# Small float32 products of three mixers, written so that neighbours stand in different column groups of the PE array

## The chip, the cores and the metric

The kernel runs on one NeuronCore of a Trainium2 chip. The metric is the device time of one execution in microseconds, the median over runs.

The engines that matter: TensorE (PE) multiplies, with its weight loads recorded apart (PEld); VectorE (DVE) and ScalarE (ACT) work on rows of 128 partitions; GpSimd (POOL) does little here; SyncE (SP) issues the DMAs. Each engine works through its own queue in order.

## The reference

Two layers; each has a half-step SwiGLU block, a mixer of three branches, a cross-attention and another half-step SwiGLU block. The sequence is 256 tokens of width 1024, all in float32. Of the mixer:

```
gla: a = where(lower, (q*eg) @ (k/eg).T, (q/eg) @ (k*eg).T)     4 heads of 32, chunks of 64 tokens
     o = a @ v + (q*eg) @ S_prev ;  S = decay * S + k.T @ v
s5:  x_t = Abar x_{t-1} + Bbar u_t ;  y_t = Re(C x_t) + D u_t    16 groups of 16 channels, 64 states
fox: p = softmax(q k.T / 8 + F_t - F_s, causal) ; o = p @ v      8 heads of 64, query blocks of 128
```

## The kernel before

Every large product is done in float32r by a high and a low part in three passes (`mm3`, L255). A weight block of 128x1024 (`wf`) is fetched by SP, split by ACT into the high part (`wh`, L237) and by DVE into the low part (`wl`, L241); seven split blocks form a ring, and `ahead` keeps it filled up to six or seven blocks ahead of PE.

The mixers and the set-up of S5 are generators, *tasks*, that are moved one step on at `tick`, `rest` or `run_tasks`, between the projections that PE works on. A `yield` ends a step. No scheduler moves instructions: their order on each engine is that in which the Python code writes them.

The small products that the change touches are plain float32 matmuls. A matmul writes to the PSUM partitions that its output tile names; partitions 0 to 31, 32 to 63, 64 to 95 and 96 to 127 belong to four column groups of the array. One such matmul stands in the program as one instruction, and in the trace as two records on PE and two on PEld.

- **S5 set-up** (`s5_setup`, during the first SwiGLU block): for each of eight pairs of groups, `cz.T @ wa` (L744), 32x128, the real and the imaginary part accumulated. All outputs stand at partitions 0 to 31, four pairs to a PSUM bank (`mm`). DVE transposes each bank in blocks of 32 into `hk` (L746), adds the D term (`dd`, L626), and four ACT copies (L753) spread `hk` over the four partition blocks of `m1`, which the mixer reads.
- **GLA** (`gla`): for each pair of chunks `pr`, the logits of a chunk (L858, two products of 64x256: `kie` with `qb[0]`, `keg` with `qb[1]`), the even chunk at partitions 0 to 63 and the odd at 64 to 127 of one bank. Then the output `po` (L884 from the state, 64x256, not for chunk 0; L887 four heads, 64x64 with 64 rows of the array), again by chunks.
- **FoX** (`fox`): seven steps for four heads. Step s does the values of head s-3 (L1071, L1072: keys 0 to 127 for all 256 queries, keys 128 to 255 for the last 128), the transposes of the softmax of head s-2 (L1059) and the logits of head s (L1040, L1041). Even heads write to partitions 0 to 63, odd ones to 64 to 127 of one bank, which is split after the odd head. A layer runs `fox` twice.

Of the kernel before, what the change touches and what calls it, by code (L numbers as in the profile page):

```python
# [8 lines left out]
F32 = mybir.dt.float32  # L9
# [24 lines left out]
WARM = 6  # L34
TAIL = 5

C_ID, C_FM, C_P2, C_HM, C_END = 0, 128, 512, 520, 524


PASSES = ((0, 0), (0, 1), (1, 0))  # L40
# [14 lines left out]
class Trunk:  # L55
# [554 lines left out]
    def s5_setup(self, l, pool):  # L610
# [8 lines left out]
        n = [0]  # L619
# [5 lines left out]
        def tt(o, x, y, op, eng=V):  # L625
            eng.tensor_tensor(o, x, y, op=op)  # L626
            return o
# [108 lines left out]
            tt(m3[:, i], (w1, w2)[i], (w2, w1)[i], (ALU.add, ALU.subtract)[i])  # L736
            yield

        hk = pool.tile([128, 8, 4, 32], F32, tag="hk", name="hk")[0:32]
        for q in range(2):  # L740
            ps = self.bank()
            for j in range(4):
                for i in range(2):
                    T.matmul(ps[0:32, j * 128:(j + 1) * 128], lhsT=cz[:, i, 4 * q + j],  # L744
                             rhs=wa[:, i, 4 * q + j].rearrange("p k h -> p (k h)"), start=i == 0, stop=i == 1)
            V.transpose(hk[:, 4 * q:4 * q + 4].rearrange("p a k h -> p (a k h)"), ps[0:32])  # L746
            yield
        dd = pool.tile([128, 8, 32], F32, tag="dd", name="dd")[0:32]
        tt(dd, self.ident[0:32, 0:32].unsqueeze(1).to_broadcast([32, 8, 32]),
           col[0:32, 32:40].unsqueeze(2).to_broadcast([32, 8, 32]), ALU.mult)  # L750
        tt(hk[:, :, 3], hk[:, :, 3], dd, ALU.add)
        for s in range(4):
            S.copy(m1[32 * s:32 * s + 32, :, 0:4 - s], hk[:, :, s:4])  # L753
        yield

        er, ei = self.er, self.ei
        V.memset(er[:, :, 0:1], 1.0)
# [60 lines left out]
    def gla(self, l, psm, vg, sgg, com, pool):  # L818
        yield from self.gla_gates(l, psm, com, pool)
        yield  # L820
        qs, ks = self.qk
        nc, ident = self.nc, self.ident
        V, S, G, T = nc.vector, nc.scalar, nc.gpsimd, nc.tensor
        eg, ieg, kd = self.ge

        def tl(shape, name):
            return pool.tile(shape, F32, tag=name, name=name)


        hm = self.cst[:, C_HM:C_HM + 4]  # L830
        kie, keg, ae = tl([128, 256], "g"), self.zeu[0][:, 0:256], tl([128, 3], "ae")
        V.tensor_tensor(kd, ks, kd, op=ALU.mult)
        V.tensor_tensor(kie, ks, ieg, op=ALU.mult)
        V.tensor_tensor(keg, ks, eg, op=ALU.mult)
        S.copy(ae, eg[:, 63:255:64])
        yield 2
        pkt = self.pbank(1)
        for t in range(2):
            T.transpose(pkt[:, t * 128:(t + 1) * 128], kd[:, t * 128:(t + 1) * 128], ident)
        kdt = tl([128, 512], "zl")[:, 0:256].rearrange("p (a b) -> p a b", a=2)  # L840
        S.copy(kdt, two(pkt[:, 0:256]))
        yield
        qb = []
        for e in (eg, ieg):
            V.tensor_tensor(e, qs, e, op=ALU.mult)
            qb.append(self.per.tile([128, 4, 256], F32, tag="nw", name="qb", bufs=2))
            V.tensor_tensor(qb[-1], e[:].unsqueeze(1).to_broadcast([128, 4, 256]),
                            hm.unsqueeze(2).to_broadcast([128, 4, 256]), op=ALU.mult)
            yield
        qf = eg  # L850
        asel = two(self.zeu[1])
        for pr in range(2):
            at = self.pbank(pr)
            for c in (2 * pr, 2 * pr + 1):
                o = slice(64 * (c % 2), 64 * (c % 2) + 64)
                cc = slice(c * 64, c * 64 + 64)
                for i, k in ((0, kie), (1, keg)):
                    T.matmul(at[o, i * 256:(i + 1) * 256], lhsT=k[:, cc], rhs=qb[i][:, :, cc], start=True, stop=True)  # L858
            S.copy(asel[:, pr], at[:, 256:512])
            V.copy_predicated(asel[:, pr], self.gmask, at[:, 0:256])  # L860
            yield

        st = [self.zeu[0][:, 0:256], self.zeu[0][:, 256:512], tl([128, 256], "g")]
        pds = self.pbank(0), self.pbank(1)
        for c in range(3):
            r = slice(64 * (c % 2), 64 * (c % 2) + 64)
            T.matmul(pds[c % 2][:, (c // 2) * 256:(c // 2) * 256 + 256], lhsT=kdt[r, c // 2], rhs=vg[r, c // 2],
                     start=True, stop=True)
        hm = hm.unsqueeze(2).to_broadcast([128, 4, 64])
        for c in range(3):  # L870
            s4 = st[c].rearrange("p (h e) -> p h e", h=4)
            V.tensor_tensor(s4, pds[c % 2][:, (c // 2) * 256:(c // 2) * 256 + 256].rearrange("p (h e) -> p h e", h=4), hm,
                            op=ALU.mult)
            if c:
                V.scalar_tensor_tensor(st[c], st[c - 1], ae[:, c:c + 1], st[c], op0=ALU.mult, op1=ALU.add)
        po = self.pbank(3)
        ggain = tl([128, 256], "scan0")
        nc.sync.dma_start(ggain, self.a["gla_norm_g"][l].partition_broadcast(128))
        yield
        for c in range(4):  # L880
            r = slice(64 * (c % 2), 64 * (c % 2) + 64)
            o = po[r, (c // 2) * 256:(c // 2) * 256 + 256]
            if c:
                T.matmul(o, lhsT=qf[:, c * 64:c * 64 + 64], rhs=st[c - 1], start=True, stop=False)  # L884
            for h in range(4):
                e = slice(h * 64, h * 64 + 64)
                T.matmul(o[:, e], lhsT=asel[r, c // 2, e], rhs=vg[r, c // 2, e], start=c == 0,  # L887
                         stop=c == 0 or h == 3)
            if c == 1:
                yield  # L890
        osq, on = tl([128, 512], "zl"), self.zeu[0]
        o8 = osq[:].rearrange("p (a b) -> p a b", a=8)
        S.activation(osq, po, AF.Square)
        ov, orr = tl([128, 8], "ov"), tl([128, 8], "orr")
        V.tensor_tensor(sgg, sgg, ggain[:].unsqueeze(1).to_broadcast([128, 2, 256]), op=ALU.mult)
        V.tensor_reduce(ov, o8, axis=AX.X, op=ALU.add)
        V.tensor_scalar(ov, ov, 1.0 / 64.0, EPS, op0=ALU.mult, op1=ALU.add)
        G.tensor_tensor(orr, ov, self.mhalf, op=ALU.pow)
        yield
        V.tensor_tensor(o8, po[:].rearrange("p (a b) -> p a b", a=8), orr[:].unsqueeze(2).to_broadcast([128, 8, 64]),  # L900
                        op=ALU.mult)
        V.scalar_tensor_tensor(on, osq, 0.5, sgg[:].rearrange("p a b -> p (a b)"), op0=ALU.mult, op1=ALU.mult)
        yield 2
        pot = self.pbank(3)
        for t in range(2):
            for k in range(2):
                T.transpose(pot[:, k * 256 + t * 128:k * 256 + t * 128 + 128],
                            on[:, t * 256 + k * 128:t * 256 + k * 128 + 128], ident)
        goh = com.tile([128, 2, 256], F32R, tag="goh", name="goh")
        gol = com.tile([128, 2, 256], F32R, tag="gol", name="gol")  # L910
        self.split_ps(goh, gol, pot)
        self.gla_out = (goh, gol, 2)
# [115 lines left out]
    def fox(self, q, fqk, fv, out, pool):  # L1028
# [31 lines left out]
            pts[i] = tl([128, 512], "ptn")[:, 0:384]  # L1060
            S.copy(pts[i], pt[:, 0:384])

        pf = [None]

        def value(i):
            if i % 2 == 0:
                pf[0] = self.bank()
            o = pf[0][64 * (i % 2):64 * (i % 2) + 64]
            c = slice((4 * q + i) * 64, (4 * q + i) * 64 + 64)
            p = pts.pop(i)  # L1070
            T.matmul(o[:, 0:256], lhsT=fv[:, 0, c], rhs=p[:, 0:256], start=True, stop=False)  # L1071
            T.matmul(o[:, 128:256], lhsT=fv[:, 1, c], rhs=p[:, 256:384], start=False, stop=True)  # L1072
            if i % 2:
                hp = (4 * q + i) // 2
                self.split_ps(out[0][:, hp], out[1][:, hp], pf[0][:, 0:256])

        for s in range(7):
            if s >= 3:
                value(s - 3)
            if 2 <= s < 6:  # L1080
                turn(s - 2)
            if s < 4:
                logits(s)
                self.n_logits = s + 1
            yield
            if s < 4:
                scale(s)
# [339 lines left out]
def _layout(inp):  # L1427
# [56 lines left out]

    pair = [4 * (j % 2) + j // 2 for j in range(8)]
    col = np.zeros((L, 128, 40), np.float32)
    col[:, 0:32, 32:40] = f["s5_d"].reshape(L, 8, 32)[:, pair].transpose(0, 2, 1)
    col[:, :, 2:4] = f["s5_glu_b"].reshape(L, 2, 128).transpose(0, 2, 1)
    col[:, :, 4] = f["gla_gate_b"]
    col[:, 32:40, 5] = f["fox_f_b"]  # L1490
# [19 lines left out]
        cst[:, C_FM + c:C_FM + c + 128] = np.where(r[:, None] >= r[None, :], 0.0, -NEG)  # L1510
    o["scan0"] = (np.arange(256) % 64 != 0).astype(np.float32)
    cst[:, C_P2:C_P2 + 8] = (2.0 ** np.arange(8))[None, :]
    cst[:, C_HM:C_HM + 4] = r[:, None] // 32 == np.arange(4)[None, :]
    o["cst"] = cst
    o["gmask"] = np.ascontiguousarray(
# [26 lines left out]
```

## Time and profile before

| | us |
|---|---|
| median of 3 runs | 1439.51 |
| lowest and highest run | 1436.96, 1439.73 |
| profiled execution, its own time | 1437.95 |
| span of its trace | 1436.1 |
| PE busy | 1419.9 (99%) |
| DVE busy | 927.3 (65%) |
| ACT busy | 712.9 (50%) |

The span runs from the first to the last instruction in the trace; the profiled execution's own time is 1.85 us longer. Busy time of PE is the union of its records, whose ends are modelled, so it hides how densely they follow each other: distances from start to start tell that. The granted TensorE clock is 0.999 of full speed over the span.

### The profile page before, as it was taken

How to read it: one execution, taken by the hardware profiler on the slowest of the kernel's cores; microseconds unless marked ns; L12 is line 12 of the kernel's file. 1: busy time of each engine (PE TensorE's matmuls, PEld its weight loads, DVE VectorE, ACT ScalarE, POOL GpSimd, SP SyncE). 2: the span in 40 equal slices, each digit the busy share in tenths (PEclk: the TensorE clock that was granted, in tenths of full speed). 3: DMA queues.
4: the chain of work that ended last, by engine and by line, in shares of the span. 5: the costliest groups of instructions: out<-in, count | busy, mean ns of one | idle time of the engine just before them, and what ended most of it. 6: DMA issues, size and time to landing. Idle time of an engine off the chain costs nothing.

```text
span 1436.1 us, 24637 instructions
## 1 busy us (share of the span) xinstructions
PE 1419.9 (99%) x9970; PEld 1308.1 (91%) x9970; DVE 927.3 (65%) x1385; ACT 712.9 (50%) x1127; POOL 60.4 (4%) x58
## 2 busy tenths in 40 slices
PE   9999999999999999999999999999999999999998
PEld 7999989899979889999999999898999898899997
DVE  6787567755587656555577775667656866665553
ACT  5444447354455546444454444463643645454442
POOL 0000000001110000000001000000013000000000
PEclk9999999999999999999999999999999999999999
DMA  7664637345556437556646556372465565375661
GB/s 276 217 199 145 213 126 208 125 155 197 171 191 233 150 118 250 188 179 189 192 152 214 179 192 190 122 237 79 147 234 177 166 231 172 101 239 183 190 187 43
DMA packets 75892, 257.00 MB, mean 179 GB/s; under 512 B 8673, under 2 KB 11777, under 8 KB 75778
## 3 DMA queue, kind: packets, MB, share of 16 engines
q1 hardware_dynamic: 75778, 255.43, 54.6%
q8 instruction: 78, 1.28, 0.4%
q14 instruction: 36, 0.29, 0.1%
HBM read 253.30 MB, written 2.10 MB: 178 GB/s over the span
## 4 chain that ended last, share of the span: by engine, by line
PE 87%; DVE 6%; ACT 3%; issue 2%; DMA 2%; POOL 0%; SPq 0%; DVEq 0%; POOLq 0%; ACTq 0%
PE mm L255 56%; PE pa L255 21%; PE mm L341 4%; DVE wl L241 1%; ACT wh L237 1%; PE mm L434 1%; DMA wf<-in_xa_k 1%; ACT junk L386 1%; DVE acc L1231 1%; PE mm L1071 1%; PE mm L744 1%; PE mm L928 1%; PE pa L963 0%; DVE xtl L1228 0%; PE pa L1059 0%
## 5 line engine op out<-in xcount | busy, mean ns | idle before, releaser
L241 DVE TENSOR_TENSOR wl<-wf,wh 128x1024 fp32r<-128x1024 f32 (+1 forms) x438 | 521.4, 1204 | 254.8 <-ACT wh L237 253.7
L255 PE MATMUL mm<-xth,wh 128*128 128x256 f32 (+1 forms) x2000 | 568.0, 284 | 0.0
L255 PE MATMUL mm<-xth,wl 128*128 128x256 f32 (+1 forms) x2000 | 566.1, 283 | 0.0
L255 PE MATMUL mm<-xtl,wh 128*128 128x256 f32 (+1 forms) x2000 | 565.2, 283 | 0.0
L237 ACT CAST wh<-wf 128x1024 fp32r<-128x1024 f32 (+1 forms) x442 | 445.9, 1029 | 145.4 <-PE mm L255 54.2
L255 PEld LDWEIGHTS mm<-xth,wh 128*128 128x128 f32 (+1 forms) x2000 | 377.2, 189 | 4.7 <-issue 2.8
L255 PEld LDWEIGHTS mm<-xtl,wh 128*128 128x128 f32 (+1 forms) x2000 | 375.5, 188 | 1.7
L255 PEld LDWEIGHTS mm<-xth,wl 128*128 128x128 f32 (+1 forms) x2000 | 376.3, 188 | 0.0
L255 PE MATMUL pa<-wh,hl 128*128 128x512 f32 x320 | 125.4, 392 | 0.0
L255 PE MATMUL pa<-wl,hh 128*128 128x512 f32 x320 | 125.2, 391 | 0.0
L255 PE MATMUL pa<-wh,hh 128*128 128x512 f32 x320 | 124.8, 390 | 0.0
L575 ACT ACTIVATE sil<-mm 128x256 f32<-128x256 f32 (+1 forms) x96 | 35.1, 366 | 117.0 <-PE mm L255 108.9
L237 ACT CAST hh<-h 128x256 fp32r<-128x256 f32 x80 | 32.5, 406 | 103.4 <-DVE h L577 103.4
L577 DVE TENSOR_TENSOR h<-sil,mm 128x256 f32<-128x256 f32 (+1 forms) x96 | 38.0, 396 | 61.0 <-ACT sil L575 61.0
L255 PEld LDWEIGHTS pa<-wh,hl 128*128 128x128 f32 x320 | 60.0, 188 | 12.8
L255 PEld LDWEIGHTS pa<-wl,hh 128*128 128x128 f32 x320 | 60.1, 188 | 11.8
L255 PEld LDWEIGHTS pa<-wh,hh 128*128 128x128 f32 x320 | 60.2, 188 | 11.7
L393 POOL TENSOR_TENSOR rr<-rv,mhalf 128x1 f32<-128x1 f32 x36 | 23.5, 653 | 960.0 <-DVE rv L392 960.0
L241 DVE TENSOR_TENSOR hl<-h,hh 128x256 fp32r<-128x256 f32 x80 | 34.1, 426 | 37.8 <-ACT hh L237 37.8
L237 ACT CAST xth<-mm 128x512 fp32r<-128x512 f32 x39 | 22.7, 588 | 54.5 <-PE mm L434 24.5
L255 PE MATMUL mm<-mt,wh 128*128 128x256 f32 x256 | 46.6, 284 | 0.0
L1186 ACT ACTIVATE gt<-mm 128x512 f32<-128x512 f32 x24 | 14.3, 598 | 61.6 <-PE mm L255 55.1
(289 smaller groups left out, 1766.4 us busy)
## 6 DMA issues: line engine op xcount, KB each, us to landing
wf<-in_ffn_gu SPq DMA_DIRECT2D x176, 512.0 KB, 4.5
wf<-in_ffn_dn SPq DMA_DIRECT2D x88, 512.0 KB, 4.4
wf<-in_w_cols SPq DMA_DIRECT2D x72, 512.0 KB, 4.9
wf<-in_w_mix SPq DMA_DIRECT2D x16, 512.0 KB, 3.9
wf<-in_xa_k SPq DMA_DIRECT2D x16, 512.0 KB, 6.1
wf<-in_xa_q SPq DMA_DIRECT2D x16, 512.0 KB, 5.8
wf<-in_xa_v SPq DMA_DIRECT2D x16, 512.0 KB, 5.9
wf<-in_xa_o SPq DMA_DIRECT2D x16, 512.0 KB, 3.9
```

The lines of the kernel that those rows point to most:

```text
L237: self.nc.scalar.copy(h, src)
L241: (eng or self.nc.vector).tensor_tensor(full(lo), src, h.bitcast(F32), op=ALU.subtract)
L255: self.nc.tensor.matmul(out, lhsT=lhs[i], rhs=rhs[j], start=start and n == 0, stop=stop and n == 2)
L341: self.nc.tensor.matmul(out, lhsT=xt[b][:, kk, tk], rhs=w[2 * g + i][a][:, k * width:(k + 1) * width], start=first, stop=last)
L386: self.nc.scalar.activation(jk, src, AF.Square, scale=math.sqrt(f / D), accum_out=s)
L393: self.nc.gpsimd.tensor_tensor(r, v, self.mhalf[:, 0:1], op=ALU.pow)
L434: self.nc.tensor.transpose(ps[:, i * 128:(i + 1) * 128], hn[:, k * 128:(k + 1) * 128], self.ident)
L575: nc.scalar.activation(sil, gate, AF.Silu)
L577: nc.vector.tensor_tensor(h, sil, up, op=ALU.mult)
L744: T.matmul(ps[0:32, j * 128:(j + 1) * 128], lhsT=cz[:, i, 4 * q + j], rhs=wa[:, i, 4 * q + j].rearrange("p k h -> p (k h)"), start=i == 0, ...
L928: T.matmul(v[:, j * 64:(j + 1) * 64], lhsT=m2[:, i, j], rhs=u4[:, j], start=j == 0, stop=j == 7)
L1071: T.matmul(o[:, 0:256], lhsT=fv[:, 0, c], rhs=p[:, 0:256], start=True, stop=False)
```

## The change

Nothing is computed otherwise; products are written in another order, and S5's set-up is laid out anew.

- S5 set-up: the 16 products go to one bank, four pairs to the four column groups in turn. The transposed result `hk` has 128 partitions and 2x4x32 columns instead of 32 and 8x4x32, DVE's operations on it are one transpose of 128x256 and two of 128x64, the D term comes from a new constant (`C_E4`, 32 more columns of `cst`), and 16 ACT copies take the place of four, four to a step.
- GLA: in a pair of chunks, the logits and the output products alternate between the two chunks.
- FoX: the values of two heads are written together, at steps 4 and 6, with alternating heads.

```diff
-        hk = pool.tile([128, 8, 4, 32], F32, tag="hk", name="hk")[0:32]
+        ps = self.bank()
         for q in range(2):
-            ps = self.bank()
-            for j in range(4):
-                for i in range(2):
-                    T.matmul(ps[0:32, j * 128:(j + 1) * 128], lhsT=cz[:, i, 4 * q + j],
-                             rhs=wa[:, i, 4 * q + j].rearrange("p k h -> p (k h)"), start=i == 0, stop=i == 1)
-            V.transpose(hk[:, 4 * q:4 * q + 4].rearrange("p a k h -> p (a k h)"), ps[0:32])
-            yield
+            for i in range(2):
+                for r in range(4):
+                    T.matmul(ps[32 * r:32 * r + 32, q * 128:(q + 1) * 128], lhsT=cz[:, i, 4 * q + r],
+                             rhs=wa[:, i, 4 * q + r].rearrange("p k h -> p (k h)"), start=i == 0, stop=i == 1)
+        hk = pool.tile([128, 2, 4, 32], F32, tag="hk", name="hk")
+        V.transpose(hk[:].rearrange("p q k h -> p (q k h)"), ps[:, 0:256])
+        yield
...
         for s in range(4):
-            S.copy(m1[32 * s:32 * s + 32, :, 0:4 - s], hk[:, :, s:4])
-        yield
+            for r in range(4):
+                S.copy(m1[32 * s:32 * s + 32, r:r + 5:4, 0:4 - s], hk[32 * r:32 * r + 32, :, s:4])
+            yield
...
-            for c in (2 * pr, 2 * pr + 1):
-                o = slice(64 * (c % 2), 64 * (c % 2) + 64)
-                cc = slice(c * 64, c * 64 + 64)
-                for i, k in ((0, kie), (1, keg)):
+            for i, k in ((0, kie), (1, keg)):
+                for c in (2 * pr, 2 * pr + 1):
+                    o = slice(64 * (c % 2), 64 * (c % 2) + 64)
+                    cc = slice(c * 64, c * 64 + 64)
                     T.matmul(at[o, i * 256:(i + 1) * 256], lhsT=k[:, cc], rhs=qb[i][:, :, cc], start=True, stop=True)
...
+        for pr in range(2):
+            cs = [(c, slice(64 * (c % 2), 64 * (c % 2) + 64)) for c in (2 * pr, 2 * pr + 1)]
+            for c, r in cs:
+                if c:
+                    T.matmul(po[r, pr * 256:pr * 256 + 256], lhsT=qf[:, c * 64:c * 64 + 64], rhs=st[c - 1],
+                             start=True, stop=False)
             for h in range(4):
                 e = slice(h * 64, h * 64 + 64)
+                for c, r in cs:
+                    T.matmul(po[r, pr * 256 + h * 64:pr * 256 + h * 64 + 64], lhsT=asel[r, pr, e], rhs=vg[r, pr, e],
+                             start=c == 0, stop=c == 0 or h == 3)
...
+        def values(i):
+            pf = self.bank()
+            ps = [pts.pop(i), pts.pop(i + 1)]
+            for n in range(2):
+                for h, p in enumerate(ps):
+                    c = slice((4 * q + i + h) * 64, (4 * q + i + h) * 64 + 64)
+                    o = pf[64 * h:64 * h + 64]
+                    T.matmul(o[:, 128 * n:256], lhsT=fv[:, n, c], rhs=p[:, 256:384] if n else p[:, 0:256],
+                             start=n == 0, stop=n == 1)
+            hp = (4 * q + i) // 2
+            self.split_ps(out[0][:, hp], out[1][:, hp], pf[:, 0:256])
 
         for s in range(7):
-            if s >= 3:
-                value(s - 3)
+            if s in (4, 6):
+                values(s - 4)
```

What stands in the queues, at three places. PE in the mixer, GLA's output for chunks 2 and 3 with FoX's logits (L1040, L1041 before, L1043, L1044 now) ahead of it, before:

```order
L1041 MATMUL pa<-fk,fq 128x256
L884 MATMUL pa<-zz,eg 64x256
L887 MATMUL pa<-vg,zz 64x64 x4
L884 MATMUL pa<-g,eg 64x256
L887 MATMUL pa<-vg,zz 64x64 x4
L255 MATMUL mm<-xth,wh 128x256
```

and now:

```order
L1044 MATMUL pa<-fk,fq 128x256
L885 MATMUL pa<-zz,eg 64x256
L885 MATMUL pa<-g,eg 64x256
L890 MATMUL pa<-vg,zz 64x64 x8
L255 MATMUL mm<-xth,wh 128x256
```

The two products from the state stand together, and the eight of 64x64 behind them, alternating between the chunks.

PE in the mixer, step 4 of the first FoX (`ptn` the transposed softmax, `lm` the softmax), between two projections, before:

```order
L255 MATMUL mm<-xth,wl 128x256
L1071 MATMUL mm<-ptn,fv 64x256
L1072 MATMUL mm<-ptn,fv 64x128
L1059 MATMUL pa<-cst,lm 128x128 x3
L255 MATMUL mm<-xth,wh 128x256
```

and now:

```order
L255 MATMUL mm<-xth,wl 128x256
L1073 MATMUL mm<-ptn,fv 64x256 x2
L1073 MATMUL mm<-ptn,fv 64x128 x2
L1062 MATMUL pa<-cst,lm 128x128 x3
L255 MATMUL mm<-xth,wh 128x256
```

Steps 4 and 6 have two heads; steps 3 and 5 lose their two matmuls and keep the rest.

ACT in the first SwiGLU block, where `m1` is filled (`m_1027`), before:

```order
L237 CAST wh<-wf 128x1024 x4
L575 ACTIVATE sil<-mm 128x256
L237 CAST hh<-h 128x256
L753 COPY m_1027<-hk 32x1024
L753 COPY m_1027<-hk 32x8x96
L753 COPY m_1027<-hk 32x8x64
L753 COPY m_1027<-hk 32x8x32
L237 CAST wh<-wf 128x1024 x2
```

and now:

```order
L237 CAST wh<-wf 128x1024 x3
L754 COPY m_1027<-hk 32x2x128 x4
L237 CAST wh<-wf 128x1024
L575 ACTIVATE sil<-mm 128x256
L237 CAST hh<-h 128x256
L754 COPY m_1027<-hk 32x2x96 x4
L237 CAST wh<-wf 128x1024
L754 COPY m_1027<-hk 32x2x64 x4
L237 CAST wh<-wf 128x1024
L575 ACTIVATE sil<-mm 128x256
L237 CAST hh<-h 128x256
L754 COPY m_1027<-hk 32x2x32 x4
```

The first copies stand one weight split earlier, the last ones several splits later, with splits between them.

## Rows read from the trace of the kernel before

**Rows 1.** The page's chain that ended last, by engine.
```profile
PE 87%; DVE 6%; ACT 3%; issue 2%; DMA 2%; POOL 0%; SPq 0%; DVEq 0%; POOLq 0%; ACTq 0%
```

**Rows 2.** Busy us of each engine (instructions) in two stretches, clock, DMA.
```profile
core 0: us, PE busy (x) PEld busy (x) DVE busy (x) ACT busy (x) POOL busy (x), PEclk, DMA share, GB/s
100.00:130.00 30.00, 30.00 (x224) 27.98 (x224) 19.30 (x52) 13.16 (x18) 0.00 (x0) 1.00 0.40 127
...
250.00:320.00 70.00, 69.68 (x511) 60.76 (x510) 48.19 (x99) 29.93 (x62) 2.01 (x1) 1.00 0.44 141
```

**Rows 3.** Whom PE waited for: us in total, times, longest.
```profile
PE pa L1040 <- DVE nm L1044: 0.4, 2, 0.2
```

**Rows 4.** Timeline of PE, FoX step 5: start, length, instruction, records.
```profile
299.90 0.28 PE L255 MATMUL mm<-xth,wl 128*128 128x256 f32 x1
300.11 0.65 PE L1071 MATMUL mm<-ptn,fv 128*64 128x256 f32 x2
...
300.91 0.55 PE L1059 MATMUL pa<-cst,lm 128*128 128x128 f32 x3
```

**Rows 5.** Timeline of PE, FoX step 2, which has no values.
```profile
283.18 0.28 PE L255 MATMUL mm<-xth,wl 128*128 128x256 f32 x1
283.30 0.49 PE L1059 MATMUL pa<-cst,lm 128*128 128x128 f32 x3
```

**Rows 6.** Timeline of PE around the first block of S5's set-up.
```profile
100.73 0.39 PE L255 MATMUL pa<-wl,hh 128*128 128x512 f32 x1
100.96 0.39 PE L255 MATMUL pa<-wh,hl 128*128 128x512 f32 x1
101.28 1.93 PE L744 MATMUL mm<-wa,s 128*32 128x128 f32 x16
103.14 0.39 PE L255 MATMUL mm<-xth,wh 128*128 128x256 f32 x1
103.37 0.28 PE L255 MATMUL mm<-xtl,wh 128*128 128x256 f32 x1
```

**Rows 7.** Timeline of PE, GLA's logits of chunks 0 and 1.
```profile
253.58 0.65 PE L858 MATMUL pa<-qb,g 128*64 128x256 f32 x2
254.35 0.43 PE L858 MATMUL pa<-qb,zz 128*64 128x256 f32 x1
254.35 0.43 PE L858 MATMUL pa<-qb,g 128*64 128x256 f32 x1
...
255.36 0.32 PE L928 MATMUL mm<-u,m 128*128 128x64 f32 x1
```

**Rows 8.** Timeline of PE, GLA's logits of chunks 2 and 3.
```profile
261.93 0.66 PE L858 MATMUL pa<-qb,g 128*64 128x256 f32 x4
262.41 0.61 PE L858 MATMUL pa<-qb,zz 128*64 128x256 f32 x4
```

**Rows 9.** Timeline of PE, GLA's output products; two narrow windows, then two wide ones.
```profile
272.65 0.51 PE L887 MATMUL pa<-vg,zz 64*64 64x64 f32 x6
...
272.89 0.28 PE L887 MATMUL pa<-vg,zz 64*64 64x64 f32 x2
...
272.49 0.67 PE L887 MATMUL pa<-vg,zz 64*64 64x64 f32 x8
273.09 0.65 PE L884 MATMUL pa<-zz,eg 128*64 128x256 f32 x2
273.67 0.68 PE L887 MATMUL pa<-vg,zz 64*64 64x64 f32 x8
274.27 0.39 PE L255 MATMUL mm<-xth,wh 128*128 128x256 f32 x1
...
277.98 0.65 PE L884 MATMUL pa<-zz,eg 128*64 128x256 f32 x2
...
280.34 0.39 PE L255 MATMUL mm<-xth,wh 128*128 128x256 f32 x1
```

**Rows 10.** Line L753: ACT durations in ns (least, median, most), forms.
```profile
L753 ACT COPY m<-hk x8: 403/726/1049, 113.8 to 825.6; 32x1024 f32<-32x1024 f32 x2, 32x768 f32<-32x768 f32 x2, 32x512 f32<-32x512 f32 x2, 32x256 f32<-32x256 f32 x2
```

**Rows 11.** Timeline of DVE while PE stands at GLA's logits of chunks 0 and 1.
```profile
253.07 1.22 DVE L847 TENSOR_TENSOR qb<-ieg,cst 128x1024 f32<-128x1024 f32 x1
```

More of the change, by code (lines that the diff above doesn't have):

```diff
@@ L35 @@
 TAIL = 5
-C_ID, C_FM, C_P2, C_HM, C_END = 0, 128, 512, 520, 524
+C_ID, C_FM, C_P2, C_HM, C_E4, C_END = 0, 128, 512, 520, 524, 556
 PASSES = ((0, 0), (0, 1), (1, 0))
@@ L737, in s5_setup @@
             yield
-        hk = pool.tile([128, 8, 4, 32], F32, tag="hk", name="hk")[0:32]
+        ps = self.bank()
         for q in range(2):
-            ps = self.bank()
-            for j in range(4):
-                for i in range(2):
-                    T.matmul(ps[0:32, j * 128:(j + 1) * 128], lhsT=cz[:, i, 4 * q + j],
-                             rhs=wa[:, i, 4 * q + j].rearrange("p k h -> p (k h)"), start=i == 0, stop=i == 1)
-            V.transpose(hk[:, 4 * q:4 * q + 4].rearrange("p a k h -> p (a k h)"), ps[0:32])
-            yield
-        dd = pool.tile([128, 8, 32], F32, tag="dd", name="dd")[0:32]
-        tt(dd, self.ident[0:32, 0:32].unsqueeze(1).to_broadcast([32, 8, 32]),
-           col[0:32, 32:40].unsqueeze(2).to_broadcast([32, 8, 32]), ALU.mult)
+            for i in range(2):
[5 more added lines that the diff above has]
+        yield
+        dd = pool.tile([128, 2, 32], F32, tag="dd", name="dd")
+        tt(dd, self.cst[:, C_E4:C_E4 + 32].unsqueeze(1).to_broadcast([128, 2, 32]),
+           col[:, 32:34].unsqueeze(2).to_broadcast([128, 2, 32]), ALU.mult)
         tt(hk[:, :, 3], hk[:, :, 3], dd, ALU.add)
         for s in range(4):
-            S.copy(m1[32 * s:32 * s + 32, :, 0:4 - s], hk[:, :, s:4])
-        yield
+            for r in range(4):
+                S.copy(m1[32 * s:32 * s + 32, r:r + 5:4, 0:4 - s], hk[32 * r:32 * r + 32, :, s:4])
+            yield
         er, ei = self.er, self.ei
@@ L879, in gla @@
         yield
[L880 to L884, printed above, removed]
+        for pr in range(2):
[4 more added lines that the diff above has]
+                             start=True, stop=False)
             for h in range(4):
                 e = slice(h * 64, h * 64 + 64)
-                T.matmul(o[:, e], lhsT=asel[r, c // 2, e], rhs=vg[r, c // 2, e], start=c == 0,
-                         stop=c == 0 or h == 3)
-            if c == 1:
+                for c, r in cs:
+                    T.matmul(po[r, pr * 256 + h * 64:pr * 256 + h * 64 + 64], lhsT=asel[r, pr, e], rhs=vg[r, pr, e],
+                             start=c == 0, stop=c == 0 or h == 3)
+            if pr == 0:
                 yield
@@ L1061, in turn @@
             S.copy(pts[i], pt[:, 0:384])
[L1063 to L1075, printed above, removed]
+        def values(i):
[9 more added lines that the diff above has]
+            self.split_ps(out[0][:, hp], out[1][:, hp], pf[:, 0:256])
         for s in range(7):
-            if s >= 3:
-                value(s - 3)
+            if s in (4, 6):
+                values(s - 4)
             if 2 <= s < 6:
@@ L1486, in _layout @@
     col = np.zeros((L, 128, 40), np.float32)
-    col[:, 0:32, 32:40] = f["s5_d"].reshape(L, 8, 32)[:, pair].transpose(0, 2, 1)
+    col[:, :, 32:34] = f["s5_d"].reshape(L, 8, 32)[:, pair].reshape(L, 2, 128).transpose(0, 2, 1)
     col[:, :, 2:4] = f["s5_glu_b"].reshape(L, 2, 128).transpose(0, 2, 1)
@@ L1512, in _layout @@
     cst[:, C_P2:C_P2 + 8] = (2.0 ** np.arange(8))[None, :]
+    cst[:, C_E4:C_E4 + 32] = r[:, None] % 32 == np.arange(32)[None, :]
     cst[:, C_HM:C_HM + 4] = r[:, None] // 32 == np.arange(4)[None, :]
```

## Prediction

> **What bounds the kernel now.** I read the chain of work that ended last first: TensorE (PE) holds 87% of it, DVE 6% and ACT 3% [rows 1]. Then the windows of the two stages that the change touches, the first feed-forward block with the S5 set-up (100 to 130 us) and the mixer (250 to 320 us): PE is busy for 30.00 of 30 us and 69.68 of 70 us, while DVE has 19.30 and 48.19 us of work there and ACT 13.16 and 29.93 [rows 2]. Then the list of who waited for whom on PE: the only wait on a line of FoX, GLA or S5 is the FoX logits' for DVE, 0.4 us in two times, 0.2 the longest [rows 3]. So in these stages nobody makes PE wait, and time taken from PE's issue comes off the end as long as the others keep up. Since the page's matmul ends are modelled, I do not count busy time but the distance from one start to the next.
>
> **How records run now.** A plain f32 matmul leaves two records. FoX's values of one head are two records of 256 columns and two of 128, one behind the other: they start 0.21 us after the last projection matmul ahead of them, and the transposes behind them 0.80 later [rows 4]. That is 1.01 us from the projection to the transposes; where a step has transposes and no values, the same distance is 0.12 [rows 5]. A head's values cost 0.89 us, part of it for the change of array shape (128x128 to 128x64 and back).
>
> The S5 set-up's products all go to PSUM partitions 0 to 31: 16 records take 1.86 us until the next projection starts, 0.116 each. From the 512-wide projection ahead (100.96) to the second one behind (103.37) 2.41 us pass, and 0.23 + 0.12 would without them (0.23 is the step from 100.73 to 100.96): 2.06 us, 0.20 of it around the block for the change of shape. There are two such blocks in a layer [rows 6].
>
> Two column groups at once occur already, in GLA's logits (L858), where chunks 0 and 1 write to partitions 0 to 63 and 64 to 127. In the first pair the second product of chunk 0 and the first of chunk 1 both start at 254.35 [rows 7]; in the second pair four records take 0.48 us until the next four start [rows 8]. One column group alone needs 0.58 for two such records (L884, 273.09 to 273.67 [rows 9]). So two groups with 128 rows each do run side by side, each at the speed it has alone.
>
> **FoX, what is saved.** Eight single values a layer become four pairs. Four events of 0.89 us go (the steps that held values 0 and 2 keep only their transposes): 3.56 us. The four that stay hold eight records where there were four, in two groups that run together; the second group's lag I put at 0.01 each. The value of an even head moves one step later, but its only reader, the split of the pair, stood at the odd head's step before and stands there still, so nothing is late next. The bank is taken one step later and held more briefly. 3.5 us a layer.
>
> **S5, what is saved.** Two blocks (4.12 us) become one of 32 records in four column groups. No row shows four groups at once: if all run together the 32 records take 8 x 0.116 = 0.93 us, if none do 3.71, and 0.20 for the shape either way. I take the first, since the nearest row, two groups, shows no loss: 4.12 - 0.93 - 0.20 = 2.99, less 0.04 for three groups' lag, 2.95 us a layer. If only two fit at once: 2.06 saved.
>
> By the Trainium skill, "TensorE: Matmul & The Clock Gate", section "The mechanism" of Part 3, a weight load overlaps matmuls in flight only when its row group differs, and products in four column groups over all 128 rows share theirs; by that rule S5 would save 0.2 a layer instead of 2.95. This trace does not agree where it can be seen: the two records at 254.35 use the same 128 rows [rows 7].
>
> The rest of the set-up: four ACT copies that take 1.05 to 0.40 us (2.9 in all) become sixteen. From the line's shortest and longest (0.403 for 256 columns, 1.049 for 1024) a copy costs 0.19 + 0.84 ns a column, so four each of 256, 192, 128 and 64 columns take 5.2 us: 2.3 more a layer, over four steps [rows 10]. ACT has 16.8 us free in those 30, and the weight blocks are split up to six ahead of PE; so nothing, and 4.6 us over both layers if that cover were gone. DVE's two transposes of 32x512 become one of 128x256, and its two further operations shrink from 256 columns to 64. The set-up ends two steps later, and what it makes is read in the mixer alone, the next stage. Nothing for these.
>
> **GLA, what is saved.** Chunks 0 and 1: 272.49 to 274.27, 1.78 us, now. After: one L884 block (0.58), then 16 records of 64x64 of which two go together, 8 steps in the 0.60 that eight take now (273.67 to 274.27), 0.01 lag: 1.19, saves 0.59. Chunks 2 and 3: 277.98 to 280.34, 2.36 us, now [rows 9]. After: the two L884 together (0.58), the pairs 0.60, lags 0.03: saves 1.15. No row shows 64x64 pairs; the bounds are this and no overlap, which costs 8 x 0.06 = 0.48 in each of the two places (four 64x64 records take from 272.65 to 272.89, 0.06 each [rows 9]); I take overlap, as the pairs share neither rows nor columns. Logits, first pair: chunk 0's second product starts at 254.35, just behind DVE's end on its input (253.07 + 1.22), and chunk 1's first stands behind it in the queue [rows 7, 11]. Written first, chunk 1's first runs during that wait, and the two others end 0.58 after 254.35, at 254.93 instead of 255.36: 0.43. The second pair already runs as two streams: nothing. Together 2.17 us a layer.
>
> **Sum.** 3.5 + 2.95 + 2.17 = 8.62 a layer, 17.2 for both layers (the second runs the same code). The profiled execution took 1437.95 us (span 1436.1 and 1.85 around it): 1420.75. The median of the runs stands 1.56 above it, 1439.51: **1422.3**.
>
> **Rivals.**
> *Records come no closer than 0.06 us on average.* That is the closest spacing of the rows I read, that of L887 [rows 9]. S5 then takes 32 x 0.06 + 0.20 = 2.12 and saves 2.00; the 64x64 pairs gain nothing and GLA saves 2.17 - 0.96 = 1.21; FoX (eight records in 0.80) is untouched. 6.7 a layer, 13.4: **1426**. For it: no row shows more than two abreast. Against: starts 0.00 apart [rows 7].
>
> *The groups do not run abreast in the new places.* What stays are the changes of shape: 0.20, as at S5, for each of four in FoX and one in S5, and three in GLA at 0.60 - 8 x 0.06 = 0.12: 1.4 a layer, 2.8: **1436.7**. Against: [rows 7, 8]. The rule of the Trainium skill cited above, from "TensorE: Matmul & The Clock Gate", would have it so.
>
> *The mixer's other engines become the bound.* If half of what FoX and GLA save (5.7 a layer) turns into waits for DVE, as the logits' 0.2 us is one already: **1428**. Against: DVE has work for 48.19 of 70 us [rows 2].
>
> *Slower:* each change of column group drains the array as a change of shape does, at 0.12. A layer has 46 more of them (12 in FoX, 15 in S5, 15 in GLA's products, 4 in its logits): 5.5 us against 1.4 saved, +8.2 in all, **1447.7**. It decides from 0.03 us a change. Against: groups alternate at no cost in [rows 7, 8]. By the Trainium skill, "TensorEngine Tiling (Array Packing)", section "Key Properties", only a change of mode drains, not one of tile; the logits agree.
>
> **Chances and range.** Forecast 0.62, the 0.06 rival 0.17, mixer 0.11, not abreast 0.06, slower 0.04. The forecast's own range is 1419 to 1425 (S5 in twos at the one end, the runs' spread of 1.5 at the other). 1418 to 1429 takes in the first rival and the mixer's. Measurement tells 0.2%, 2.9 us, from no change: faster 0.92, same 0.04 (part of the not-abreast case lies there), slower 0.04.
>
> **What would show it.** Right: one block of 32 L743 records that ends about 1.0 us after its start; 16 L890 records in 0.6; eight L1073 records in 0.8 at four places a layer; four L858 g records first in both pairs; PE's list of waits as short as now. Wrong: L743 starts 0.06 or 0.116 apart on average; new waits of PE for DVE on the logits or transposes of FoX, or for split weights in 100 to 130 us.

## The result, and the profile after

The changed kernel takes 1420.24 us (median of 4 runs, 1419.17 to 1423.85) beside 1438.57 for the kernel before on the same chips: a ratio of 0.9878, 95% interval 0.9866 to 0.9889. That is 18.3 us less (by the interval 16.0 to 19.3); 17.2 were forecast, and 1422.3 us with a range of 1418 to 1429. The median of the kernel before is that of four runs here, so it differs from the 1439.51 of three runs. The span of the profiled execution fell from 1436.1 to 1418.7 us, by 17.4.

The rows of PE in the changed kernel that answer to [rows 6], the S5 set-up, in order of time:

```profile
100.52 0.39 PE L255 MATMUL pa<-wh,hl 128*128 128x512 f32 x1
100.84 1.08 PE L743 MATMUL mm<-wa,s 128*32 128x128 f32 x32
101.85 0.39 PE L255 MATMUL mm<-xth,wh 128*128 128x256 f32 x1
102.07 0.28 PE L255 MATMUL mm<-xtl,wh 128*128 128x256 f32 x1
```

All 32 records lie between 100.84 and 101.85: 1.01 us, where two blocks of 16 had 1.86 each. From 100.52 to 102.07 it is 1.55 us, 1.20 more than without the block. Four groups run abreast.

GLA's logits of chunks 0 and 1, which answer to [rows 7]:

```profile
249.86 0.40 PE L255 MATMUL mm<-wh,xtl 128*128 128x512 f32 x1
250.19 0.65 PE L859 MATMUL pa<-qb,g 128*64 128x256 f32 x4
250.97 0.65 PE L859 MATMUL pa<-qb,zz 128*64 128x256 f32 x4
251.55 0.32 PE L931 MATMUL mm<-u,m 128*128 128x64 f32 x1
```

The four `g` records of both chunks stand together now, PE then waits (0.78 us from the first `g` to the first `zz`, where four records take 0.48 in [rows 8]), and the `zz` follow in 0.58. The block takes 1.36 us instead of 1.78.

GLA's output, chunks 0 and 1 and then 2 and 3, which answers to [rows 9]:

```profile
268.65 0.65 PE L885 MATMUL pa<-zz,eg 128*64 128x256 f32 x2
269.23 0.68 PE L890 MATMUL pa<-vg,zz 64*64 64x64 f32 x16
269.84 0.39 PE L255 MATMUL mm<-xth,wh 128*128 128x256 f32 x1
...
273.54 0.43 PE L885 MATMUL pa<-zz,eg 128*64 128x256 f32 x1
273.55 0.43 PE L885 MATMUL pa<-g,eg 128*64 128x256 f32 x1
273.81 0.38 PE L885 MATMUL pa<-zz,eg 128*64 128x256 f32 x1
273.82 0.38 PE L885 MATMUL pa<-g,eg 128*64 128x256 f32 x1
274.13 0.68 PE L890 MATMUL pa<-vg,zz 64*64 64x64 f32 x16
274.74 0.39 PE L255 MATMUL mm<-xth,wh 128*128 128x256 f32 x1
```

Sixteen 64x64 records take the 0.61 us that eight took. The two blocks fill 1.19 and 1.20 us instead of 1.78 and 2.36; the two L885 start 0.01 apart.

FoX, step 4 with two heads, and step 5, which has none now and answers to [rows 4]:

```profile
289.23 0.28 PE L255 MATMUL mm<-xth,wl 128*128 128x256 f32 x1
289.44 0.87 PE L1073 MATMUL mm<-ptn,fv 128*64 128x256 f32 x8
290.24 0.55 PE L1062 MATMUL pa<-cst,lm 128*128 128x128 f32 x3
...
293.36 0.28 PE L255 MATMUL mm<-xth,wl 128*128 128x256 f32 x1
293.47 0.49 PE L1062 MATMUL pa<-cst,lm 128*128 128x128 f32 x3
293.72 0.36 PE L255 MATMUL mm<-xth,wh 128*128 128x256 f32 x1
```

Two heads take from 289.44 to 290.24, 0.80, as one did in [rows 4]. In the kernel before, the projection behind step 5 stood here:

```profile
301.21 0.36 PE L255 MATMUL mm<-xth,wh 128*128 128x256 f32 x1
```

That step took 1.31 us from 299.90 to 301.21, and takes 0.36 now, from 293.36 to 293.72.

Whom PE waited for in the changed kernel (us in total, times, longest), which answers to [rows 3]:

```profile
PE mm L434 <- DVE nw L427: 5.6, 5, 2.9
...
PE pa L1043 <- DVE nm L1047: 0.4, 2, 0.2
PE mm L341 <- DVE wl L241: 0.3, 1, 0.3
```

FoX's logits wait as much as before. New is one wait of 0.3 us for a low weight part, outside the changed blocks. The longest wait at L434, in the first layer, is 2.9 us where it was 2.2.

### The profile page after: what moved, and what is told of

Same layout as the page of the kernel before. It is cut to its first block, busy times and chain, and to the rows that moved or that the text cites. A ratio compares the mean times of both kernels' runs of the same rounds, so it can differ in the third digit from the quotient of the medians.

```text
span 1418.7 us, 24657 instructions
## 1 busy us (share of the span) xinstructions
PE 1402.0 (99%) x9970; PEld 1296.2 (91%) x9970; DVE 924.2 (65%) x1383; ACT 717.2 (51%) x1151; POOL 60.3 (4%) x58
## 4 chain that ended last, share of the span: by engine, by line
PE 88%; DVE 6%; ACT 3%; issue 2%; DMA 0%; POOL 0%; DVEq 0%; POOLq 0%; ACTq 0%
PE mm L255 57%; PE pa L255 21%; PE mm L341 4%; DVE wl L241 2%; PE mm L434 1%; ACT wh L237 1%; ACT junk L386 1%; DVE acc L1232 1%; PE mm L931 1%; PE pa L966 0%; DVE xtl L1229 0%; DMA wf<-in_xa_k 0%; PE mm L1073 0%; PE pa L1044 0%; PE pa L1062 0%
```

## The experiments

### One part at a time

Three kernels, each the kernel before with one part of the diff alone.

FoX's part:

```diff
         for s in range(7):
-            if s >= 3:
-                value(s - 3)
+            if s in (4, 6):
+                values(s - 4)
```

> The kernel before with FoX's part alone. Theory (PE's issue is the bound and column groups run side by side): four events of 0.89 us a layer go, 3.5 us a layer, 7.0 in all, so about 1431.5 us beside a before of 1438.6. Rival (the mixer's other engines take back half): 3.5 in all. Rival (values of two heads run one behind the other): about 1.6 in all.

Measured: 1430.2 us beside 1437.99, ratio 0.9949 (0.9935 to 0.9963), 7.8 us less. PE's list of waits has one of 0.6 us here that the kernel before does not have, for DVE at GLA's logits (L858); the changed kernel's list does not have it either.

S5's set-up:

```diff
-                    T.matmul(ps[0:32, j * 128:(j + 1) * 128], lhsT=cz[:, i, 4 * q + j],
...
+                    T.matmul(ps[32 * r:32 * r + 32, q * 128:(q + 1) * 128], lhsT=cz[:, i, 4 * q + r],
```

> The kernel before with S5's set-up alone. Theory: two blocks that cost 2.06 us become one of 1.2, 2.9 a layer, 5.9 in all, and the ACT copies cost nothing: about 1432.7. Rival (the 16 ACT copies delay the weight splits and PE waits for them): up to 4.6 less is saved. Rival (only two groups abreast): 4.1 in all.

Measured: 1432.06 us, ratio 0.9958 (0.9946 to 0.9971), 5.9 us less.

GLA's part:

```diff
-            for c in (2 * pr, 2 * pr + 1):
...
+            for i, k in ((0, kie), (1, keg)):
...
             for h in range(4):
...
+                for c, r in cs:
```

> The kernel before with GLA's part alone. Theory: 1.74 us a layer from the output products, 0.43 from the first pair of logits, 4.3 in all: about 1434.2; together with the two other parts 17.2, the whole change. Rival (the parts hide one another's waits): the three parts' sum differs from the whole by more than 2 us.

Measured: 1433.53 us, ratio 0.9968 (0.9955 to 0.998), 4.5 us less.

The three add up to 18.2 us, and the whole change saved 18.3: nothing shows that a part hides or takes back what another gives. That the two figures are so close is partly luck, since each part is known to within 2 us by its interval. The rival with the mixer's other engines leaves 3.5 us of FoX's saving and 2.2 of GLA's; the intervals are 5.3 to 9.3 and 2.9 to 6.5, so it is out. Each part came within 0.8 us of its own sum.

### Does the order within a step matter?

The changed kernel with the same column groups, banks and steps, but each group's products in one run:

```diff
-        for q in range(2):
-            for i in range(2):
-                for r in range(4):
+        for r in range(4):
+            for q in range(2):
+                for i in range(2):
...
-            for n in range(2):
-                for h, p in enumerate(ps):
+            for h, p in enumerate(ps):
+                for n in range(2):
```

The first cut is S5's, the second FoX's. GLA's logits went back to the order of the kernel before, and L890's loops over heads and chunks were exchanged.

> The changed kernel with the same column groups, banks and steps, but each group's products written in one run and not in turn (S5: eight records of one group, then the next group; FoX: head by head; GLA's heads and logits: chunk by chunk). Theory A (PE runs each column group by itself and looks past any number of records that wait): S5's block stays at 1.0 us, GLA's pairs at 0.6, FoX's at 0.8; only the first logits lose their 0.43 a layer, +0.9 in all. Theory B (it looks past some four records, as the logits of the kernel before show): S5's block takes some 20 steps of 0.116, 2.3 us, each GLA pair 0.2 more, FoX the same: +4.4 in all. Theory C (strict order, abreast only when neighbours differ): S5's block 3.5 us, GLA's blocks 1.1, FoX's 1.3: +11 in all.

Measured: 1425.51 us, ratio to the kernel before 0.9912 (0.9898 to 0.9926), 5.3 us more than the changed kernel's 1420.24, which was timed beside other runs of the kernel before (5.8 by the two ratios). PE of this kernel at S5's block, as seen in three windows that end at 101.32, at 101.34 and behind the block (a row counts the records that its window holds):

```profile
100.86 0.62 PE L743 MATMUL mm<-wa,s 128*32 128x128 f32 x4
...
100.86 0.76 PE L743 MATMUL mm<-wa,s 128*32 128x128 f32 x6
...
100.86 2.46 PE L743 MATMUL mm<-wa,s 128*32 128x128 f32 x32
103.25 0.39 PE L255 MATMUL mm<-xth,wh 128*128 128x256 f32 x1
```

Four records of the first group have started by 101.32, and two more by 101.34: its fifth and the first of the next group. So the next group came in when three records of the first were still waiting, and the block took 2.39 us, the 2.3 of theory B. The first logits, the 64x64 blocks and FoX:

```profile
251.57 0.65 PE L859 MATMUL pa<-qb,g 128*64 128x256 f32 x2
...
253.37 0.32 PE L931 MATMUL mm<-u,m 128*128 128x64 f32 x1
...
271.05 0.96 PE L890 MATMUL pa<-vg,zz 64*64 64x64 f32 x16
271.94 0.39 PE L255 MATMUL mm<-xth,wh 128*128 128x256 f32 x1
...
291.78 0.88 PE L1073 MATMUL mm<-ptn,fv 128*64 128x256 f32 x8
292.59 0.55 PE L1062 MATMUL pa<-cst,lm 128*128 128x128 f32 x3
```

L890, in runs of eight, 0.89 instead of 0.61; FoX, in runs of four, 0.81 instead of 0.80. The first pair of logits is back at 1.8 us (251.57 to 253.37). By layer S5 loses 1.38 us, the two L890 blocks 0.28 each, the first logits 0.43 and FoX 0.03 over its four places: 4.8 over both layers of the 5.3 measured. Theory B holds, A and C fall: a run of four costs next to nothing, a run of eight does.

### Is it a queue for each group, or one for all?

The changed kernel with S5's two matmuls of a group, four records, in one run, then the next group:

```diff
-            for i in range(2):
-                for r in range(4):
+            for r in range(4):
+                for i in range(2):
```

> The changed kernel with S5's products ordered so that a group has its two matmuls (four records) in one run, then the next group. In the grouped order a new group started when three records of the one before it were still waiting. If each column group has a queue of its own of some four records, all four groups start together: block 1.0 us. If three waiting records in all are what PE looks past, only two groups run at once: about 1.9 us (16 steps of 0.109 and the start).

PE in this kernel, a window that ends at 101.29 and one over the block:

```profile
101.24 0.34 PE L743 MATMUL mm<-wa,s 128*32 128x128 f32 x4
...
101.24 1.12 PE L743 MATMUL mm<-wa,s 128*32 128x128 f32 x32
102.28 0.38 PE L255 MATMUL mm<-xth,wh 128*128 128x256 f32 x1
```

Four records start within 0.05 us of each other, so all four groups are at work while three records of each of the first three wait; the block takes 1.04 us. So what holds the next group back is a queue for each group, not three waiting records in all.

The one run of this kernel took 1423.22 us. The span of its trace, 1421.4, is 2.7 longer than that of the changed kernel, and the block accounts for 0.03 a layer of it. Counted record by record along PE, 0.4 us more arise at the start of the kernel, 0.7 near 415 us and 1.7 near 1119 us. There the granted TensorE clock differs (columns as in [rows 2], the clock is the third figure from the end); two stretches of this kernel, then the same two of the changed kernel:

```profile
416.00:420.00 4.00, 4.00 (x21) 3.60 (x20) 2.71 (x7) 1.76 (x4) 0.55 (x1) 0.60 0.00 0
1120.00:1125.00 5.00, 5.00 (x35) 5.00 (x35) 3.33 (x7) 3.24 (x7) 1.10 (x2) 0.76 0.00 0
...
416.00:420.00 4.00, 3.88 (x31) 3.73 (x32) 3.37 (x7) 1.65 (x4) 0.55 (x1) 1.00 0.00 0
1120.00:1125.00 5.00, 5.00 (x44) 5.00 (x44) 3.33 (x7) 4.16 (x7) 0.55 (x1) 1.00 0.02 5
```

PE had waited for DVE at L434 just before, 2.0 and 1.9 us long; in the changed kernel it waited 2.9 us at the first of these places and the clock stayed up. So the longer time says nothing against runs of four.

### Two groups instead of four

The changed kernel with S5's products in two column groups, in turn (the copies and the D term laid out to match):

```diff
-                    T.matmul(ps[32 * r:32 * r + 32, q * 128:(q + 1) * 128], lhsT=cz[:, i, 4 * q + r],
...
+                        T.matmul(ps[64 * g:64 * g + 32, o:o + 128], lhsT=cz[:, i, j],
```

> The changed kernel with S5's 32-column products in two column groups (partitions 0 to 31 and 64 to 95) instead of four, written in turn. If four groups run as freely as two: the block of 32 records takes 16 steps of 0.109, about 1.9 us, against 1.01 with four, so +0.9 a layer, +1.8 in all. If four groups shared something that two do not: the four-group steps would be longer than 0.109, and here below 1.9 us would not follow; a step shorter than 0.109 here would show that.

The timeline of PE in this kernel:

```profile
101.17 1.94 PE L745 MATMUL mm<-wa,s 128*32 128x128 f32 x32
103.04 0.39 PE L255 MATMUL mm<-xth,wh 128*128 128x256 f32 x1
```

1.87 us against 1.01 with four groups: 16 steps of 0.117 here, 8 of 0.126 there, with the start of the block in both. Inside both blocks, from the second step on, a step starts 0.109 us behind the one before, as in the single group of the kernel before: two more streams make a step no longer. The one run took 1421.51 us, 1.3 more than the changed kernel where 1.8 were expected. In its trace the block adds 0.86 us in each layer, and the longest wait at L434 is 1.9 us instead of 2.9, which takes part of that back.

### Do the ACT copies cost anything?

The changed kernel with each of the sixteen copies written twice:

```diff
             for r in range(4):
-                S.copy(m1[32 * s:32 * s + 32, r:r + 5:4, 0:4 - s], hk[32 * r:32 * r + 32, :, s:4])
+                for _ in range(2):
+                    S.copy(m1[32 * s:32 * s + 32, r:r + 5:4, 0:4 - s], hk[32 * r:32 * r + 32, :, s:4])
```

> The changed kernel with each of S5's 16 ACT copies written twice, same data: 5 us more of ACT work a layer in the first feed-forward block. Theory (the split weight blocks lie far enough ahead): PE's waits stay as they are, 0.0 within the measurement. Rival (ACT's copies delay the splits, and the 2.3 us that the change adds a layer cost time already): up to 10 us slower, with new waits of PE for the high or low weight parts between 100 and 130 us.

Measured: 1420.54 us, ratio to the kernel before 0.9877 (0.986 to 0.9893), beside 0.9878 of the changed kernel. ACT's groups from 95 to 130 us, first of the changed kernel (busy us, mean ns of one, idle before):

```profile
L754 ACT COPY m<-hk 32x256 f32<-32x256 f32 (+3 forms) x16 | 5.2, 323 | 3.8 <-DVE hk L626 3.6
```

and of this one:

```profile
L755 ACT COPY m<-hk 32x256 f32<-32x256 f32 (+3 forms) x32 | 10.3, 323 | 4.3 <-DVE hk L626 3.6
```

The changed kernel's copies take the 5.2 us that were estimated, and 5.1 more a layer cost nothing that can be measured.

### What do the first logits wait for?

The changed kernel with DVE's second operand for GLA's logits made in two halves, the columns of chunks 0 and 1 first:

```diff
-            V.tensor_tensor(qb[-1], e[:].unsqueeze(1).to_broadcast([128, 4, 256]),
-                            hm.unsqueeze(2).to_broadcast([128, 4, 256]), op=ALU.mult)
+            for hf in range(2):
+                s = slice(128 * hf, 128 * hf + 128)
+                V.tensor_tensor(qb[-1][:, :, s], e[:, s].unsqueeze(1).to_broadcast([128, 4, 128]),
+                                hm.unsqueeze(2).to_broadcast([128, 4, 128]), op=ALU.mult)
```

> The changed kernel with GLA's second moving operand of the logits built in two halves, columns of chunks 0 and 1 first. Theory (the first pair's second products wait for DVE's one operation over all 256 columns): the step from the first to the second product in the first pair falls from 0.78 to 0.48 us, 0.3 a layer. Rival (they wait for something else): 0.78 stays.

The timeline of PE in this kernel:

```profile
250.11 0.65 PE L861 MATMUL pa<-qb,g 128*64 128x256 f32 x4
250.59 0.60 PE L861 MATMUL pa<-qb,zz 128*64 128x256 f32 x4
```

0.48 us from `g` to `zz`: the wait is gone, and it was for that operation. Over both layers this is worth 0.6 us by these distances, below what the runs can tell. The one run took 1421.04 us; its granted clock was 0.59 from 416 to 420 us, where the changed kernel had 1.00, so whether the kernel is faster as a whole is not shown.

## Why the prediction was right

**PE's issue is the bound, so time taken from it comes off the end.** Shown: the parts' savings (7.8, 5.9, 4.5 us) are those of their PE blocks and add up to the whole. Counted record by record, PE gets 8.7 us ahead of the kernel before in the stretch from 90 to 373 us, which holds the first layer's changed blocks, and 8.8 from 767 to 1053 us, which holds the second's (times of the changed kernel); 8.62 were forecast for each. The longer wait at L434 takes 0.7 of it back. The rival of the mixer's other engines falls; PE's waits at FoX's logits are 0.4 us as before. The forecast time of 1422.3 us is 2.1 above the median: 0.9 of that is the median of the kernel before, which was 1439.51 then and is 1438.57 now, and 1.1 the saving.

One step of this reading was too simple. The list of waits [rows 3] does not show every wait: the first logits stood for DVE, as the prediction's own working for GLA says, and no line of the list has it. The wait is about 0.3 us, and the records' modelled ends cover most of it.

**FoX, 3.5 us a layer.** The mechanism was right and the term a little small. 0.89 was the distance up to the transposes. With the values gone the transposes themselves are shorter too: from the first of them to the projection behind, 0.30 us in the kernel before (300.91 to 301.21) and 0.25 now (293.47 to 293.72). So step 5 lost 1.31 - 0.36 = 0.95 and not 0.89. The four places lose 0.94 to 0.95 each, and the second heads' lag takes 0.03 back: 3.7 a layer, 7.5 in all. FoX alone measured 7.8, in an interval of 5.3 to 9.3.

**S5, 2.95 us a layer.** 4.12 became 1.20, a saving of 2.92. That four groups run as freely as two was the open bound, taken from two groups without a row of its own; the block of 1.01 us and the two-group kernel's 1.87 settle it. The ACT copies were free, as their doubling shows.

**GLA, 2.17 us a layer.** The output gave 0.59 and 1.16, the first logits 0.42. That pairs of 64x64 overlap was the other open bound; they do. The reason given for the first logits, that chunk 1's first product stood in the queue behind a waiting one, is borne out by the grouped kernel, which has the old order of the logits and lost that saving again, and the wait itself was for DVE, as the kernel with the halved operand shows.

**The other rivals.** Records do come closer than 0.06 us on average: 32 in 1.01 us is 0.032, 16 in 0.61 is 0.038. A change of column group costs nothing that can be seen: neighbours start 0.01 apart, and a block of two groups takes what one took. By the Trainium skill, "TensorE: Matmul & The Clock Gate", section "The mechanism" of Part 3, weight loads overlap matmuls in flight only from another row group. S5's and FoX's blocks use the same 128 rows in all their groups and run abreast (32 records in 1.01 us, eight in 0.80), so for column groups the measurement decides against that sentence.

**What was not foreseen** changed nothing in the sum: the prediction takes products written in turn and does not ask whether the order matters. For FoX the placing of two heads in one step is enough (0.81 against 0.80); for S5 (2.39 against 1.01) and L890 (0.89 against 0.61) the order matters, since their runs of eight hold the next group back.

## What to carry to other kernels

When PE is the bound and a stage issues small products with 32 or 64 output columns, put them in one step, with outputs at different column groups: two or four then run in about the time of one, and a block merged into another saves the time at its two edges besides (about 0.20 us at S5). Write them in turn, or in runs of no more than four records (two plain f32 matmuls) per group; and put a product that may wait for another engine behind those of the other groups that need not. Measure distances from start to start, with what lies on both sides of a block: PE's busy share is 99% before and after, and the list of waits left out one of 0.3 us.

## What the runs showed of the hardware

A column group seems to have a queue of its own: in runs of eight records the next group starts when three of the run are still waiting, in runs of four all four groups start within 0.05 us. Only runs of four and of eight were tried, with f32 products of 32 and 64 columns; what the queue counts, records or matmuls, these runs do not tell apart, and that it is a queue is read from these starts. The description of the engines ahead says that each works through its own queue in order; for the starts of PE's records that does not hold. In the grouped S5 block the second group's first record starts at 101.33, ahead of the sixth to eighth of the first group (101.43 to 101.65; the groups are told apart by the spacing of their records). Four streams of 128 rows each need as long for a step as two and as one: 8 steps in 1.01 us, 16 in 1.87, and 16 records of one group in 1.86.
